# The delta rule's merge gates in column pairs: seven block products for three of eight k-tile pairs, in turn with the up blocks

## Chip, cores and metric

One core of one Trainium2 chip runs the whole program. The metric is device time in microseconds (us) of that core, given as the median of several executions; one further execution was taken with the hardware profiler, and all rows below come from it.

## What is computed

One layer of a hybrid decoder trunk over 256 tokens, width 2048, in float32. Cut to what matters here:

```
xn = RMSNorm(x)                      z = xn @ W_in
y_m = mLSTM(z_m)   y_r = RWKV7(z_r)  y_s = S5(z_s)
mixed = sig(g_m)*(y_m @ U_m) + sig(g_r)*(y_r @ U_r) + sig(g_s)*(y_s @ U_s)
h = x + mixed @ W_out
h = h + (silu(hn @ W_g) * (hn @ W_u)) @ W_d          # hn = RMSNorm(h)
h = h + (p @ W_ple) * sig(RMSNorm(h) @ W_pg)         # then a last RMSNorm
```

The change is about `g_r`, the 2048 gate columns of z that weigh the delta rule's (RWKV7's) branch. They are one product of a 256x2048 activation with a 2048x2048 weight.

## The kernel before

Every large product is done in two parts per operand: an operand is split into a rounded high part (a ScalarE copy) and the rest (a VectorE subtraction), and three TensorE matmuls (high by high, low by high, high by low) stand for one product. Weights come in chunks of four 128x512 tiles, 1 MB each, in the fixed order of `wall` through a ring of three `raw` tiles on SP's DMA queue; `chunk` splits a chunk into two pairs of `whi` and `wlo` tiles, of which there are three each, under high priority. `gemm_tm` makes one block of 512 output columns for both halves of the tokens (`t` is 0 or 1): for each of 16 k-tiles and each half three matmuls of 128x512, so 24 matmuls a chunk, into two PSUM tiles of the pool `mm` (four tiles). Everything else that TensorE writes (the small products and the transposes) goes into PSUM tiles of the pool `sm` (`psm()`, four tiles as well).

SBUF tiles of one tag share a number of buffers: `t2` has 16 of 128x512 (`b2`), `t8` two of 128x2048 (`b8`; at this place `KR` and then `UV`), `t4` twelve (`b4`), and the pool `pb` one each of `Dm`, `cm`, `X`, `XT` and `Y`, used by `rw_inverse` alone.

The order on each engine is made at build time by a planner, which follows the order of the program as a priority, but lets an instruction of a later part go first where the earlier part waits. So the serial chain of the delta rule (`rw_kappa`, `rw_gram`, `rw_inverse`, four `rw_chunk`, `rw_norm`) is written ahead of the gates of `s` and `r`, and runs in small pieces between their matmuls. `rw_chunk` takes `pu`, `py`, `px` and (except in the last) `pst` from `sm`; `rw_norm` takes two `pq` (L1072) and two `pt` (L1079), and ends with `yrh` and `yrl`, which `up("r", n)` needs. Per block, `up` multiplies the gate with a product of four k-tiles and adds it to `mixed`; the result is transposed through `sm` and split into `mh` and `ml` for W_out.

The feed-forward part already does, for the gate and up columns of W_g and W_u, what the change does for `g_r`: for k-tile pairs u in `SEVEN` it replaces the eight block products of a 2x2 by 2x2 block scheme by seven products of sums (Strassen's scheme in Winograd's form). `seven()` makes the sums of weight blocks on GpSimd and VectorE and splits them, and the products that belong to several outputs are gathered in four more PSUM tiles, `M[1]`, `M[7]`, `M[5]` and `M[6]`, of the pool `sm`, from the first of these pairs to the last:

```
ORDER = (3, 4, 0, 5, 1, 6, 2, 7)
SEVEN = (0, 1, 2)
...
    if u == SEVEN[0]:
        for q in (1, 7, 5, 6):
            M[q] = psm("M%d" % q)
```

A pair of this kind takes 7 x 3 = 21 matmuls, any other 24.

Of the kernel before, what the change touches and what calls it, by code (L numbers as in the profile page):

```python
# [74 lines left out]
def trunk(ctx: ExitStack, tc: tile.TileContext, xT, x, pT, wall, vecs, csts, s5b, s5c, gfin, out, dbg=None):  # L75
# [142 lines left out]
    def tt(o, a, b, op):  # L218
        nc.vector.tensor_tensor(out=o, in0=a, in1=b, op=op)
# [513 lines left out]
    def z_gate(key, n):  # L733
        ps = gemm_tm(xh, xl, NKT)
        with tc.high_priority():
            for t in range(2):
                g_ = t2("gate")
                act_fn(g_, ps[t], AF.Tanh, scale=hrs0[:, t:t + 1])
                gates[key, t, n] = g_

    def up(key, n, hi, lo, nkt, first):
# [396 lines left out]
    for n in range(4):  # L1138
        z_gate("s", n)
        up("s", n, lambda k: G["ysh"][:, k, :], lambda k: G["ysl"][:, k, :], 4, False)  # L1140
    for n in range(4):
        z_gate("r", n)
    mT = {}
    for n in range(4):
        up("r", n, lambda k: G["yrh"][:, k, :], lambda k: G["yrl"][:, k, :], 4, False)
        mh = t4v(4, "mh").bitcast(F32R)
        ml = t4v(4, "ml").bitcast(F32R)
        mT[n] = (mh, ml)
        for b in range(2):
            pt = tposed([mixed[t, n] for t in range(2)], 2 * b)  # L1150
            split(mh[:, 2 * b:2 * b + 2, :], ml[:, 2 * b:2 * b + 2, :], bank2(pt), 0.5)
# [49 lines left out]
    SF = {}
    for u in SEVEN:
        af = t2("af").rearrange("p (a t) -> p a t", a=2)  # L1210
        sf = t2("sf").rearrange("p (a t) -> p a t", a=4)
        tt(af, hh[:, 2 * u:2 * u + 2, :].bitcast(F32), hl[:, 2 * u:2 * u + 2, :].bitcast(F32), ALU.add)
        tt(sf[:, 0], af[:, 0, TS[1]], af[:, 1, TS[1]], ALU.add)
        tt(sf[:, 1], sf[:, 0], af[:, 0, TS[0]], ALU.subtract)
        tt(sf[:, 2], af[:, 0, TS[0]], af[:, 0, TS[1]], ALU.subtract)
        tt(sf[:, 3], af[:, 1, TS[0]], sf[:, 1], ALU.subtract)
        SF[u] = tuple(gu.tile([128, 4, 128], F32R, name=q + "%d" % u) for q in ("sh", "sl"))
        split(*SF[u], sf)

    def tiled(r):  # L1220

        n = r.shape[1]
        hi = ring.tile([128, 2, 512], F32R, name="whi", tag="whi", bufs=3)[:, 0:n]
        lo = ring.tile([128, 2, 512], F32R, name="wlo", tag="wlo", bufs=3)[:, 0:n]
        split(hi, lo, r)
        return [(hi[:, q], lo[:, q]) for q in range(n)]

    def seven():

        if not loaded:  # L1230
            load()
        raw, _ = loaded.pop(0)
        with tc.high_priority():
            ts_ = gu.tile([128, 3, 512], F32, name="tsum", tag="tsum", bufs=2)
            out_ = [tiled(raw[:, 0:2])]
            nc.gpsimd.tensor_tensor(out=ts_[:, 0], in0=raw[:, 3], in1=raw[:, 0], op=ALU.subtract)
            tt(raw[:, 3], raw[:, 2], raw[:, 3], ALU.subtract)
            out_.append(tiled(raw[:, 2:4]))
            tt(ts_[:, 1], raw[:, 3], raw[:, 0], ALU.add)
            nc.gpsimd.tensor_tensor(out=ts_[:, 2], in0=raw[:, 1], in1=ts_[:, 1], op=ALU.subtract)  # L1240
            out_ += [tiled(ts_[:, 0:2]), tiled(ts_[:, 2:3])]
        return out_

    def A(u, t, k):
        return hh[:, 2 * u + k, TS[t]], hl[:, 2 * u + k, TS[t]]

    for b in range(11):
        M = {q: pmm() for q in (2, 4, 3, 8)}
        done = set()

        def prods(ops, last):

            n_ = {q: max(i for i, o in enumerate(ops) if o[0] == q) for q in {o[0] for o in ops}}
            for part in range(2):
                for i, (q, a, w) in enumerate(ops):
                    mm2(M[q], *a, *w, part, q not in done, last and part == 1 and i == n_[q], True)
                    if part == 0:
                        done.add(q)

        for i, u in enumerate(ORDER):  # L1260
            last = u == ORDER[-1]
            if u in SEVEN:
                if u == SEVEN[0]:
                    for q in (1, 7, 5, 6):
                        M[q] = psm("M%d" % q)
                (b11, b21), (b22, t3), (t1, t2_), (t4_,) = seven()
                S = [tuple(SF[u][q][:, i_, :] for q in range(2)) for i_ in range(4)]
                end = u == SEVEN[-1]
                prods([(1, A(u, 0, 0), b11)], end)
                prods([(2, A(u, 0, 1), b21)], last)  # L1270
                prods([(3, S[3], b22)], last)
                prods([(7, S[2], t3)], end)
                prods([(5, S[0], t1)], end)
                prods([(6, S[1], t2_)], end)
                prods([(4, A(u, 1, 1), t4_)], last)
                if end:

                    with tc.high_priority():
                        m1, u2, u3, u4, v4 = (t2(q) for q in ("m1s", "u2", "u3", "u4", "v4"))
                        nc.scalar.copy(out=m1, in_=M[1])  # L1280
                        tt(u2, M[6], m1, ALU.add)
                        tt(u3, M[7], u2, ALU.add)
                        tt(u4, M[5], u2, ALU.add)
                        tt(v4, M[5], u3, ALU.add)
            else:
                b11, b21, b22, b12 = chunk()
                prods([(2, A(u, 0, 0), b11), (4, A(u, 1, 0), b11), (2, A(u, 0, 1), b21), (4, A(u, 1, 1), b21)], last)
                prods([(3, A(u, 0, 0), b12), (8, A(u, 1, 0), b12), (3, A(u, 0, 1), b22), (8, A(u, 1, 1), b22)], last)
        with tc.high_priority():
            for o, q in ((m1, 2), (u3, 4), (u4, 3), (v4, 8)):  # L1290
                tt(o, M[q], o, ALU.add)
        sg = []
        for t, (g_, u_) in enumerate(((m1, u4), (u3, v4))):
# [93 lines left out]
def layout(i):  # L1387
# [62 lines left out]
    wg, wu = (a[q][0].reshape(8, 2, 128, FFN) for q in ("ffn_w_gate", "ffn_w_up"))  # L1450
    for n in range(11):
        c = slice(n * 512, (n + 1) * 512)
        for u in ORDER:
            chunks.append(np.stack([wg[u, 0, :, c], wg[u, 1, :, c], wu[u, 1, :, c], wu[u, 0, :, c]], axis=1).reshape(128, 2048))
    blocks(a["ffn_w_down"][0])
    wp = a["ple_w_proj"][0]
    for n in range(4):
# [42 lines left out]
```

## Time and profile before

| | |
|---|---|
| median of 3 runs | 1662.36 us (1661.29 to 1663.82) |
| the profiled execution | 1665.54 us |
| its span, first to last instruction | 1663.8 us |
| mean granted TensorE clock | 0.997 |
| busy: TensorE, VectorE, ScalarE, GpSimd | 1643.1, 1269.2, 911.3, 173.5 us |
| mean DMA rate | 189 GB/s |

Times in a row are us from the start of the span, unless marked ns. L and a number is a line of the kernel before. A duration of a matmul is its time through the array, which overlaps the next one; the pace is the distance between starts. A merged row (x4) has its first start and the length of the whole. What stands in square brackets is the idle time of the engine ahead of the instruction and what ended it.

### The profile page before, as it was taken

The page shows a single profiled execution, that of the slowest core. Times are in us where ns is not written, and L with a number is a line of the kernel's source. Part 1 is how long each engine was busy: PE and PEld are TensorE (multiplying, and loading weights), DVE is VectorE, ACT ScalarE, POOL GpSimd, SP SyncE. Part 2 cuts the span into 40 slices and gives each one's busy share as a digit, 9 for nine tenths or more (in the row PEclk, how much of TensorE's full clock was granted, in tenths as well). Part 3 has the DMA queues.
Part 4 walks back from the last instruction along what each step waited for, and adds up shares of the span by engine and source line. Part 5 has one row for each costly group of instructions (what it writes and reads, how often), then busy time and mean ns, then how long its engine had stood idle before and what let it go on. Part 6 is the DMA issues. An engine that isn't in the chain of part 4 may idle for free. (4 is left out here: it accounts for less than half of the span.)

```text
span 1663.8 us, 23495 instructions
## 1 busy us (share of the span) xinstructions
PE 1643.1 (99%) x9255; PEld 1383.7 (83%) x9255; DVE 1269.2 (76%) x1566; ACT 911.3 (55%) x1142; POOL 173.5 (10%) x131
## 2 busy tenths in 40 slices
PE   8999999999999999999999999999999999999997
PEld 7999879988788878888888888888888888888886
DVE  6999776969988546565588889898888867666565
ACT  6465466556645444444555555555555656655454
POOL 1100100100000000000032222222222000000000
PEclk9999999999999999999999999999999999999999
DMA  9655444654554444555544555555555655555653
GB/s 356 197 174 177 160 162 177 191 189 170 188 177 152 154 153 154 183 197 200 202 174 181 203 202 203 202 190 191 193 189 198 230 186 199 181 199 184 220 186 119
DMA packets 49455, 313.69 MB, mean 189 GB/s; under 512 B 5824, under 2 KB 9152, under 8 KB 12736
## 3 DMA queue, kind: packets, MB, share of 16 engines
q1 hardware_dynamic: 43488, 304.59, 50.7%
q0 software_dynamic: 3840, 3.15, 1.1%
q10 hardware_dynamic: 2016, 4.46, 0.8%
q8 instruction: 72, 1.18, 0.3%
q14 instruction: 39, 0.32, 0.1%
HBM read 306.93 MB, written 2.10 MB: 186 GB/s over the span
## 5 line engine op out<-in xcount | busy, mean ns | idle before, releaser
L129 DVE TENSOR_TENSOR wlo<-raw,whi 128x1024 fp32r<-128x1024 f32 (+1 forms) x496 | 631.1, 1280 | 252.2 <-ACT whi L128 222.1
L128 ACT CAST whi<-raw 128x1024 fp32r<-128x1024 f32 (+1 forms) x496 | 517.7, 1049 | 553.9 <-PE mm L143 402.6
L143 PE MATMUL mm<-whi,alo 128*128 128x512 f32 x512 | 202.0, 394 | 0.0
L142 PE MATMUL mm<-whi,ahi 128*128 128x512 f32 x512 | 201.7, 394 | 0.0
L142 PE MATMUL mm<-whi,hhi 128*128 128x512 f32 x506 | 199.2, 394 | 0.4 <-ACT whi L193 0.2
L143 PE MATMUL mm<-whi,hlo 128*128 128x512 f32 x506 | 196.9, 390 | 0.0
L149 PE MATMUL mm<-ahi,whi 128*128 128x256 f32 x576 | 143.4, 286 | 7.8 <-ACT whi L128 7.8
L145 PE MATMUL mm<-wlo,hhi 128*128 128x512 f32 x506 | 146.0, 392 | 0.1
L150 PE MATMUL mm<-alo,whi 128*128 128x256 f32 x576 | 142.8, 285 | 0.3 <-DVE alo L197 0.3
L145 PE MATMUL mm<-wlo,ahi 128*128 128x512 f32 x512 | 139.6, 393 | 0.0
L142 PE MATMUL mm<-whi,dh 128*128 128x512 f32 x352 | 130.4, 390 | 0.0
L143 PE MATMUL mm<-whi,dl 128*128 128x512 f32 x352 | 130.2, 389 | 0.0
L149 PEld LDWEIGHTS mm<-ahi,whi 128*128 128x128 f32 x576 | 111.4, 194 | 8.9 <-ACT whi L128 8.1
L142 PEld LDWEIGHTS mm<-whi,hhi 128*128 128x128 f32 x506 | 95.0, 188 | 25.1 <-issue 4.1
L143 PEld LDWEIGHTS mm<-whi,alo 128*128 128x128 f32 x512 | 96.6, 189 | 21.1 <-issue 1.2
L142 PEld LDWEIGHTS mm<-whi,ahi 128*128 128x128 f32 x512 | 96.4, 188 | 21.3 <-issue 1.2
L145 PEld LDWEIGHTS mm<-wlo,ahi 128*128 128x128 f32 x512 | 96.0, 189 | 20.8 <-issue 0.4
L150 PEld LDWEIGHTS mm<-alo,whi 128*128 128x128 f32 x576 | 111.3, 194 | 0.9 <-DVE alo L197 0.5
L145 PEld LDWEIGHTS mm<-wlo,hhi 128*128 128x128 f32 x506 | 94.1, 188 | 20.1 <-DVE wlo L129 1.0
L143 PEld LDWEIGHTS mm<-whi,hlo 128*128 128x128 f32 x506 | 95.1, 188 | 18.7
L193 ACT CAST whi<-raw 128x1024 fp32r<-128x1024 f32 x66 | 69.3, 1050 | 66.9 <-DVE wlo L129 33.4
L145 PE MATMUL mm<-wlo,dh 128*128 128x512 f32 x352 | 95.9, 391 | 0.0
(532 smaller groups left out, 2779.0 us busy)
## 6 DMA issues: line engine op xcount, KB each, us to landing
raw<-in_wall SPq DMA_DIRECT2D x283, 1024.0 KB, 4.8
xrow<-in_x SPq DMA_DIRECT2D x2, 1024.0 KB, 9.6
h<-in_x ACTq DMA_DIRECT2D x8, 256.0 KB, 3.2
xraw<-in_xT SPq DMA_DIRECT2D x3, 512.0 KB, 11.0
ub<-Bh POOLq DMA_DIRECT2D x16, 64.0 KB, 3.8
ub<-uh POOLq DMA_DIRECT2D x16, 64.0 KB, 3.8
gft<-in_gfin ACTq DMA_DIRECT2D x1, 1024.0 KB, 7.0
out_dram<-fin SPq DMA_DIRECT2D x4, 256.0 KB, 3.2
```

The lines of the kernel that those rows point to most:

```text
L128: nc.scalar.copy(out=hi[:, q, :], in_=r)
L129: nc.vector.tensor_tensor(out=lo[:, q, :], in0=r, in1=hi[:, q, :].bitcast(F32), op=ALU.subtract)
L142: nc.tensor.matmul(ps, ah, wh, start=first, stop=False, skip_group_check=skip)
L143: nc.tensor.matmul(ps, al, wh, start=False, stop=False, skip_group_check=skip)
L145: nc.tensor.matmul(ps, ah, wl, start=False, stop=last, skip_group_check=skip)
L149: nc.tensor.matmul(ps, wh, ah, start=first, stop=False, skip_group_check=skip)
L150: nc.tensor.matmul(ps, wh, al, start=False, stop=False, skip_group_check=skip)
L193: nc.scalar.copy(out=hi, in_=src)
```

## The change

`gemm_pair` is the feed-forward part's block taken out as a function, with the sums of activations (`sums_of`), the weights' sums (`seven`) and the seven products beside it; the feed-forward part now calls it. `z_gate2("r", n, XS)` uses it for the gates of two blocks of 512 columns, `n` and `n + 1`, instead of `z_gate("r", n)` for one. The order of the program becomes: the sums `XS` of the activations for three k-tile pairs, gates of blocks 0 and 1, up of 0 and 1, gates of 2 and 3, up of 2 and 3; before it was gates 0 to 3, then up 0 to 3. The weights lie in `wall` in that order. The sums of activations are kept in `rw_inverse`'s buffers of `pb`, the sums of weights in `t8` buffers. The number of chunks and bytes is the same.

```
+    def room_pb(i):
+        t_ = [G["pb"].tile([128, 512], F32, name="sx", tag=q) if q else t2("sx") for q in (("Dm", "cm"), ("X", "XT"), ("Y", None))[i]]
+        return tuple(q.rearrange("p (a t) -> p a t", a=4).bitcast(F32R) for q in t_)
+    def tsum_t8():
+        return t8("tsum").rearrange("p a t -> p (a t)")[:, 0:1536].rearrange("p (a t) -> p a t", a=3)
...
+    def seven(room):
...
+            ts_ = room()
+            out_ = [tiled(raw[:, 0:2])]
+            nc.gpsimd.tensor_tensor(out=ts_[:, 0], in0=raw[:, 3], in1=raw[:, 0], op=ALU.subtract)
+            tt(raw[:, 3], raw[:, 2], raw[:, 3], ALU.subtract)
+            out_.append(tiled(raw[:, 2:4]))
+            tt(ts_[:, 1], raw[:, 3], raw[:, 0], ALU.add)
+            nc.gpsimd.tensor_tensor(out=ts_[:, 2], in0=raw[:, 1], in1=ts_[:, 1], op=ALU.subtract)
+            out_ += [tiled(ts_[:, 0:2]), tiled(ts_[:, 2:3])]
...
+    def gemm_pair(A, S, order, by7, room, prep=None, onto=None):
+        M = {q: pmm() for q in (2, 4, 3, 8)}
...
+            if u in by7:
+                if u == by7[0]:
+                    for q in (1, 7, 5, 6):
+                        M[q] = psm("M%d" % q)
+                (b11, b21), (b22, t3), (t1, t2_), (t4_,) = seven(room)
+                end = u == by7[-1]
+                prods([(1, A(u, 0, 0), b11)], end)
+                prods([(2, A(u, 0, 1), b21)], last)
+                prods([(3, S(u, 3), b22)], last)
+                prods([(7, S(u, 2), t3)], end)
+                prods([(5, S(u, 0), t1)], end)
+                prods([(6, S(u, 1), t2_)], end)
+                prods([(4, A(u, 1, 1), t4_)], last)
...
+    def z_gate2(key, n, sf):
+        c4 = gemm_pair(act_of(ahi, alo), sum_of(sf), ORDER, SEVEN, tsum_t8)
+        with tc.high_priority():
+            for o, (t, m) in zip(c4, ((0, n), (1, n), (0, n + 1), (1, n + 1))):
+                act_fn(o, o, AF.Tanh, scale=hrs0[:, t:t + 1])
+                gates[key, t, m] = o
...
-    for n in range(4):
-        z_gate("r", n)
+    XS = {u: sums_of(ahi[:, 2 * u:2 * u + 2, :], alo[:, 2 * u:2 * u + 2, :], room_pb(u)) for u in SEVEN}
     mT = {}
     for n in range(4):
+        if n % 2 == 0:
+            z_gate2("r", n, XS)
         up("r", n, lambda k: G["yrh"][:, k, :], lambda k: G["yrl"][:, k, :], 4, False)
...
-    blocks(w_in[:, 8648:10696])
-    blocks(a["w_up_r"][0])
+    for n in (0, 1024):
+        pair(w_in[:, 8648 + n:9160 + n], w_in[:, 9160 + n:9672 + n], ORDER)
+        blocks(a["w_up_r"][0][:, n:n + 1024])
```

## Rows read from the trace of the kernel before

**Rows 1.** Busy time of each engine in stretches of 20 us around the gates of `r` (length; then PE, PEld, DVE, ACT and POOL busy us with their instructions; granted TensorE clock, DMA share, GB/s).

```profile
640.00:660.00 20.00, 20.00 (x113) 16.00 (x112) 12.71 (x14) 8.97 (x12) 2.05 (x1) 1.00 0.38 130
...
740.00:760.00 20.00, 20.00 (x101) 16.66 (x100) 16.06 (x21) 9.39 (x12) 0.00 (x0) 1.00 0.47 170
```

**Rows 2.** TensorE's instructions in order of time at the start of the gates of `r` (start, length, engine, line): the first matmul of the block `r`, 0; two first matmuls of half chunks of 12 matmuls; the pieces of the delta rule's last chunk between them; and the last pair of transposes of `rw_norm`.

```profile
625.16 0.39 PE L142 MATMUL mm<-whi,ahi 128*128 128x512 f32 x1
...
632.49 0.39 PE L142 MATMUL mm<-whi,ahi 128*128 128x512 f32 x1
...
635.21 0.39 PE L142 MATMUL mm<-whi,ahi 128*128 128x512 f32 x1
...
636.21 1.15 PE L1017 MATMUL sm<-ST,KR 64*64 64x64 f32 x32
637.29 0.69 PE L1023 MATMUL sm<-UV,GB 128*64 128x64 f32 x16
...
639.86 0.40 PE L142 MATMUL mm<-whi,ahi 128*128 128x512 f32 x1
...
642.91 0.68 PE L1035 MATMUL sm<-Up,NX 64*64 64x64 f32 x16
643.52 1.99 PE L1072 MATMUL sm<-mur,ct 128*128 128x256 f32 x8
...
667.40 2.08 PE L1079 MATMUL sm<-ct,Yr 64*64 64x64 f32 x64
```

**Rows 3.** The same chain on ScalarE, in order of time.

```profile
638.02 0.37 ACT L1031 COPY Up<-sm 128x256 f32<-128x256 f32 x1 [2.42 <-PE sm L1023]
...
643.64 0.37 ACT L1036 COPY UV<-sm 64x256 f32<-64x256 f32 x1 [0.70 <-PE sm L1035]
...
649.83 0.37 ACT L1052 COPY Yr<-sm 128x256 f32<-128x256 f32 x1 [1.61 <-PE sm L1023]
...
653.01 1.06 ACT L225 ACTIVATE ysq<-Yr 128x1024 f32<-128x1024 f32 x1 [0.78 <-DVE Yr L219]
...
674.42 1.05 ACT L193 CAST yrh<-yrF 128x1024 fp32r<-128x1024 f32 x1 [0.90 <-DVE yrF L219]
```

**Rows 4.** The same chain on VectorE, in order of time.

```profile
650.23 1.22 DVE L1058 TENSOR_REDUCE st<-Yr 128x16 f32<-128x1024 f32 x1 [0.76 <-ACT Yr L1052]
651.48 0.17 DVE L214 TENSOR_SCALAR st<-st 128x16 f32<-128x16 f32 x1
651.69 1.23 DVE L219 TENSOR_TENSOR Yr<-Yr,st 128x1024 f32<-128x1024 f32 x1
...
655.29 1.21 DVE L1063 TENSOR_REDUCE st<-ysq 128x16 f32<-128x1024 f32 x1
...
661.77 1.23 DVE L219 TENSOR_TENSOR Yr<-Yr,grs 128x1024 f32<-128x1024 f32 x1
...
675.50 1.23 DVE L194 TENSOR_TENSOR yrl<-yrF,yrh 128x1024 fp32r<-128x1024 f32 x1
```

**Rows 5.** GpSimd's instructions in order of time: the clearing of `UV`, the power in `rw_norm`, and the first sum of weights of the feed-forward part.

```profile
520.82 1.95 POOL L900 MEMSET UV<- 64x1024 f32 x2 [151.23 <-PE sm L896]
657.95 3.79 POOL L1066 TENSOR_TENSOR grs<-st,nhalf 128x16 f32<-128x16 f32 x1 [135.18 <-ACT whi L128]
839.18 1.29 POOL L1236 TENSOR_TENSOR tsum<-raw 128x512 f32<-128x512 f32 x1 [177.44 <-PE mm L145]
```

**Rows 6.** The instructions that write or read a tile, with minimum, median and maximum of their ns, and the first and last start: `mur` from 480 us on, and `muv` in the whole span.

```profile
L1072 PE MATMUL sm<-mur,ct x8: 379/379/483, 643.5 to 645.1; 128*128 128x256 f32 x8
L222 DVE SCALAR_TENSOR_TENSOR mur<-mur,vt,muk x4: 478/478/484, 505.0 to 506.2; 128x256 f32<-128x256 f32 x4
...
L906 PE MATMUL sm<-ct,muv x64: 218/218/267, 522.2 to 524.1; 64*64 64x64 f32 x64
...
L222 DVE SCALAR_TENSOR_TENSOR muv<-zp,vt,muv x4: 478/479/480, 343.6 to 346.6; 128x256 f32<-128x256 f32 x4
```

**Rows 7.** The chain that ended last, in order of time (start, us, what): the same merged piece of two successive blocks of the feed-forward part, each with three pairs by seven products.

```profile
860.79 0.91 PE mm L145 x4
...
903.52 0.91 PE mm L145 x4
```

**Rows 8.** Groups of VectorE instructions in one such block, 860 to 903 us (line, engine, operation, shapes, count; busy us, mean ns; idle time before them).

```profile
L194 DVE TENSOR_TENSOR wlo<-raw,whi 128x1024 fp32r<-128x1024 f32 x6 | 8.2, 1379 | 1.0 <-PE mm L145 1.0
L194 DVE TENSOR_TENSOR wlo<-tsum,whi 128x1024 fp32r<-128x1024 f32 (+1 forms) x6 | 6.4, 1077 | 2.0 <-PE mm L145 1.9
L219 DVE TENSOR_TENSOR raw<-raw 128x512 f32<-128x512 f32 x3 | 2.1, 685 | 1.2 <-POOL tsum L1236 1.2
L219 DVE TENSOR_TENSOR tsum<-raw 128x512 f32<-128x512 f32 x3 | 2.0, 681 | 0.0
```

**Rows 9.** The one stretch after the start with a low granted clock (columns as in rows 1).

```profile
165.00:170.00 5.00, 5.00 (x18) 3.77 (x17) 3.88 (x8) 0.28 (x1) 0.00 (x0) 0.75 0.64 210
170.00:172.00 2.00, 2.00 (x9) 1.33 (x8) 0.32 (x1) 1.59 (x2) 0.00 (x0) 0.78 0.00 0
```

**Rows 10.** TensorE in order of time around the same stretch.

```profile
164.13 1.99 PE L644 MATMUL sm<-gw,sel 4*128 4x256 f32 x8
...
168.02 0.63 PE L143 MATMUL mm<-whi,alo 128*128 128x512 f32 x1
168.45 0.63 PE L142 MATMUL mm<-whi,ahi 128*128 128x512 f32 x1
```

More of the change, by code (lines that the diff above doesn't have):

```diff
@@ L197, in split, with sums, sums_of @@
             nc.vector.scalar_tensor_tensor(out=lo, in0=src, scalar=gain, in1=hi.bitcast(F32), op0=ALU.mult, op1=ALU.subtract)
+    def sums(sf, a):
+        tt(sf[:, 0], a[:, 0, TS[1]], a[:, 1, TS[1]], ALU.add)
+        tt(sf[:, 1], sf[:, 0], a[:, 0, TS[0]], ALU.subtract)
+        tt(sf[:, 2], a[:, 0, TS[0]], a[:, 0, TS[1]], ALU.subtract)
+        tt(sf[:, 3], a[:, 1, TS[0]], sf[:, 1], ALU.subtract)
+    def sums_of(hi, lo, room):
+        af = t2("af").rearrange("p (a t) -> p a t", a=2)
+        sf = t2("sf").rearrange("p (a t) -> p a t", a=4)
+        tt(af, hi.bitcast(F32), lo.bitcast(F32), ALU.add)
+        sums(sf, af)
+        split(*room, sf)
+        return room
@@ new lines, in room_of, with tsum_of @@
+    def room_of(pool, name):
+        return tuple(pool.tile([128, 4, 128], F32R, name=name + q) for q in ("h", "l"))
+    def room_pb(i):
+        t_ = [G["pb"].tile([128, 512], F32, name="sx", tag=q) if q else t2("sx") for q in (("Dm", "cm"), ("X", "XT"), ("Y", None))[i]]
+        return tuple(q.rearrange("p (a t) -> p a t", a=4).bitcast(F32R) for q in t_)
+    def tsum_of(pool):
+        return lambda: pool.tile([128, 3, 512], F32, name="tsum", tag="tsum", bufs=2)
+    def tsum_t8():
+        return t8("tsum").rearrange("p a t -> p (a t)")[:, 0:1536].rearrange("p (a t) -> p a t", a=3)
@@ new lines, in tiled @@
+    def tiled(r):
+        n = r.shape[1]
+        hi = ring.tile([128, 2, 512], F32R, name="whi", tag="whi", bufs=3)[:, 0:n]
+        lo = ring.tile([128, 2, 512], F32R, name="wlo", tag="wlo", bufs=3)[:, 0:n]
+        split(hi, lo, r)
+        return [(hi[:, q], lo[:, q]) for q in range(n)]
+    def seven(room):
+        if not loaded:
+            load()
+        raw, _ = loaded.pop(0)
+        with tc.high_priority():
[7 more added lines that the diff above has]
+            out_ += [tiled(ts_[:, 0:2]), tiled(ts_[:, 2:3])]
+        return out_
@@ new lines, in act_of, with sum_of, prods @@
+    def act_of(hi, lo):
+        return lambda u, t, k: (hi[:, 2 * u + k, TS[t]], lo[:, 2 * u + k, TS[t]])
+    def sum_of(sf):
+        return lambda u, i: tuple(q[:, i, :] for q in sf[u])
+    def gemm_pair(A, S, order, by7, room, prep=None, onto=None):
+        M = {q: pmm() for q in (2, 4, 3, 8)}
+        done = set()
+        def prods(ops, last):
+            n_ = {q: max(i for i, o in enumerate(ops) if o[0] == q) for q in {o[0] for o in ops}}
+            for part in range(2):
+                for i, (q, a, w) in enumerate(ops):
+                    mm2(M[q], *a, *w, part, q not in done, last and part == 1 and i == n_[q], True)
+                    if part == 0:
+                        done.add(q)
+        for u in order:
+            last = u == order[-1]
+            if prep is not None:
+                prep(u)
+            if u in by7:
[11 more added lines that the diff above has]
+                prods([(4, A(u, 1, 1), t4_)], last)
+                if end:
+                    with tc.high_priority():
+                        m1, u2, u3, u4, v4 = (t2(q) for q in ("m1s", "u2", "u3", "u4", "v4"))
+                        nc.scalar.copy(out=m1, in_=M[1])
+                        tt(u2, M[6], m1, ALU.add)
+                        tt(u3, M[7], u2, ALU.add)
+                        tt(u4, M[5], u2, ALU.add)
+                        tt(v4, M[5], u3, ALU.add)
+                    res = (m1, u3, u4, v4)
+                    if onto is not None:
+                        for o, r in zip(onto, res):
+                            tt(o, o, r, ALU.add)
+                        res = onto
+            else:
+                b11, b21, b22, b12 = chunk()
+                prods([(2, A(u, 0, 0), b11), (4, A(u, 1, 0), b11), (2, A(u, 0, 1), b21), (4, A(u, 1, 1), b21)], last)
+                prods([(3, A(u, 0, 0), b12), (8, A(u, 1, 0), b12), (3, A(u, 0, 1), b22), (8, A(u, 1, 1), b22)], last)
+        with tc.high_priority():
+            for o, q in zip(res, (2, 4, 3, 8)):
+                tt(o, M[q], o, ALU.add)
+        return res
@@ L739, in z_gate @@
                 gates[key, t, n] = g_
+    def z_gate2(key, n, sf):
+        c4 = gemm_pair(act_of(ahi, alo), sum_of(sf), ORDER, SEVEN, tsum_t8)
+        with tc.high_priority():
+            for o, (t, m) in zip(c4, ((0, n), (1, n), (0, n + 1), (1, n + 1))):
+                act_fn(o, o, AF.Tanh, scale=hrs0[:, t:t + 1])
+                gates[key, t, m] = o
     def up(key, n, hi, lo, nkt, first):
@@ L1199, in trunk @@
     hh, hl = hT
[L1208 to L1242, printed above, removed]
@@ L1244, in A @@
-    def A(u, t, k):
-        return hh[:, 2 * u + k, TS[t]], hl[:, 2 * u + k, TS[t]]
-    for b in range(11):
[L1248 to L1291, printed above, removed]
@@ L1292, in trunk @@
+    SF = {u: sums_of(hh[:, 2 * u:2 * u + 2, :], hl[:, 2 * u:2 * u + 2, :], room_of(gu, "sf%d" % u)) for u in SEVEN}
+    for b in range(11):
+        c11, c21, c12, c22 = gemm_pair(act_of(hh, hl), sum_of(SF), ORDER, SEVEN, tsum_of(hid_p))
         sg = []
-        for t, (g_, u_) in enumerate(((m1, u4), (u3, v4))):
+        for t, (g_, u_) in enumerate(((c11, c12), (c21, c22))):
             s_ = t2("sg")
@@ L1430, in blocks, with pair @@
             block(w[:, n * 512:(n + 1) * 512])
+    def pair(l, r, order):
+        l, r = (q.reshape(-1, 2, 128, 512) for q in (l, r))
+        for u in order:
+            chunks.append(np.stack([l[u, 0], l[u, 1], r[u, 1], r[u, 0]], axis=1).reshape(128, 2048))
     block(w_in[:, 6088:6600])
@@ L1446, in layout @@
         block(a["w_up_s"][0][:, n * 512:(n + 1) * 512])
-    blocks(w_in[:, 8648:10696])
-    blocks(a["w_up_r"][0])
+    for n in (0, 1024):
+        pair(w_in[:, 8648 + n:9160 + n], w_in[:, 9160 + n:9672 + n], ORDER)
+        blocks(a["w_up_r"][0][:, n:n + 1024])
     blocks(a["w_out"][0])
-    wg, wu = (a[q][0].reshape(8, 2, 128, FFN) for q in ("ffn_w_gate", "ffn_w_up"))
     for n in range(11):
         c = slice(n * 512, (n + 1) * 512)
-        for u in ORDER:
-            chunks.append(np.stack([wg[u, 0, :, c], wg[u, 1, :, c], wu[u, 1, :, c], wu[u, 0, :, c]], axis=1).reshape(128, 2048))
+        pair(a["ffn_w_gate"][0][:, c], a["ffn_w_up"][0][:, c], ORDER)
     blocks(a["ffn_w_down"][0])
```

## The prediction

> **What bounds the kernel now.** I read the page first: TensorE is busy 99% of the span, no other engine over 76%. So a change is worth what it takes from TensorE's own list, less what it makes TensorE wait. The table by stretches then shows the stage itself: around the gates of `r` TensorE is busy 20.00 of 20 us, VectorE 12.7 and, among the up blocks, 16.1 [rows 1]. There is no idle time to win here, and any wait put in is paid in full. TensorE's order of time gives the pace: twelve 128x512 matmuls from 632.49 to 635.21 us, 0.2267 us each, so 5.44 us for a chunk of 24 [rows 2].
>
> The reader should see in the same rows what lies between these matmuls. The gates of `r` begin at 625.16 us, while the delta rule's chain is in its last chunk. Its pieces are short, but each waits for a ScalarE or VectorE step and then for the matmuls queued ahead of it: the copy of `Up` ends at 638.39 and L1035, which needs it, starts at 642.91, 4.5 us later [rows 2, 3]. The transposes of `rw_norm` (L1079) start at 667.40, and `yrl`, the last thing that the up blocks need, is done at 676.7 [rows 2, 4]. Before, that is early: four gate blocks come first. The gates of `r` are what fills TensorE while the chain runs.
>
> **The change part by part.**
>
> *Matmuls.* Two column pairs, each with three k-tile pairs at 21 instead of 24: 2 x 3 x 3 = 18 matmuls fewer, 18 x 0.2267 = **4.08 us less** [rows 2]. Nothing excludes the full gain: the feed-forward part does 183 such matmuls and eight transposes in 42.73 us a block [rows 7], where 183 x 0.2267 is 41.5, so the seven products run at the same pace.
>
> *The place of the four extra sums.* `M[1]`, `M[7]`, `M[5]`, `M[6]` come from the pool `sm`, which is also that of the chain. What matters is whether they may have a free tile while earlier parts of the program have not yet asked for theirs. The trace answers by tiles that were ready long before. L1072 needs only `mur`, written by 506.7 us, and a tile of `sm`; it ran at 643.52, straight behind L1035, which writes the last `sm` tile that the program asks for ahead of it. L906 needs only `muv`, written by 347.1 us, and ran at 522.2 [rows 2, 6]. Both have precedence over the gates' matmuls, and both let gate matmuls pass for over 100 us. I read this as: tiles of one pool are handed out in program order. (Not in order of age, though: `UV` waited 151 us for L896, the last reader of `BK`, and so took `BK`'s place and not `KR`'s [rows 5].) Then `M[1]` cannot be had before the second pair of `rw_norm`'s `pt` tiles is, that is before L1079.
>
> *What TensorE has left to do.* Chunks 3 and 4 of the first pair take the place of the first two chunks of `r`, 0, and end at 639.86 as those do [rows 2]. Of the chunk u=0, `M[2]` and `M[3]` can go, 6 matmuls, 1.36 us. `M[1]` waits, and holds the first of three `whi`/`wlo` pairs; `M[7]` holds the second, `M[5]` and `M[6]` the third, so `M[4]` has no weights, and neither has any later chunk. The up blocks need `yrh`. TensorE stands until the chain gets to L1079, apart from the chain's own pieces.
>
> *How long.* With TensorE empty the chain has no queue to wait in. `Up` ends at 638.4 [rows 3]; L1035 behind the rest of chunk 4 and `M[2]`, 640.5 to 641.2; the copies into `UV`, 0.4, hidden behind L1072's 2.0, to 643.2; L1023, 0.69, to 643.9; `Yr`, 0.37, to 644.3. Then `rw_norm`: 1.22 + 0.17 + 1.23 on VectorE, 1.06 on ScalarE, 1.21 + 0.17 on VectorE, 3.79 on GpSimd, 1.23 on VectorE, 10.08 in all [rows 3 to 5], and some 0.6 for the hand-overs (the gaps in these rows are 0.03 to 0.23): L1079 at 655.0. From 639.86 to there is 15.1 us, in which TensorE has 1.36 of the gates and 0.68 + 1.99 + 0.69 of the chain, 4.7 in all. **10.4 us idle.** Lower bound: L1035 starts as soon as `Up` is there and L1072 slips behind, L1079 at 651, 6.4 idle. Upper bound: the planner leaves the chain the waits that it has now; the last VectorE step ends at 663.0 [rows 4], 18.4 idle. I take 10.4, since the waits of now are made by matmuls that are then not there.
>
> *The clock behind the idle time.* The one low stretch of the trace follows eight thin matmuls (L644, 4 rows): matmuls start 0.43 us apart, the clock is at 1.2 GHz for part of it, 0.75 over 5 us and 0.78 over 2 us [rows 9, 10]. That lost 5 x 0.25 + 2 x 0.22 = 1.7 us. Eleven idle us are at least as quiet, so I take **1.7**, between 0 (no fall) and 3.4 (the doubled stretch). The Trainium skill says so in general (TensorE: Matmul & The Clock Gate, "HAM oscillation"): a wait between bursts of matmuls sends the array back to half rate and the next burst starts cold. By that rule the 1.7 is due, and the change's 18 saved matmuls are worth little beside one such wait; without a fall the sum would be 1.7 lower. No trace so far shows a wait of this kind.
>
> *Restart.* The third weight pair is free only after `M[5]` and `M[6]`; `M[4]`'s weights need a copy and a subtraction behind `M[1]`, while `M[7]`, `M[5]`, `M[6]` give 2 us of cover. **0.5**, from 0 to 2.
>
> *Edits at nothing.* A chunk of seven products costs VectorE (8.2 + 6.4 + 2.1 + 2.0) / 3 = 6.2 us [rows 8], some 3.8 more than a plain one: six of them 22 us over some 108 us, in which it idles 4 to 7 of every 20 [rows 1]. The sums `XS` (per pair two operations of 0.69 and four a quarter the size [rows 8]) fall under matmuls ahead of 639 us, since `rw_inverse`'s buffers are long free. The eight adds of 0.69 behind each pair lie under chunk 7 and the up blocks. If that cover goes, each us is paid once; behind the second pair, where VectorE is at 16 of 20 [rows 1], I allow up to 2 and take 0. GpSimd's sums, 1.29 each [rows 5], meet an engine that idled 135 us before the power; one of them could delay that power by 1.3, inside the upper bound. The first needs `KR`'s buffer, free at 637.4 after L1017 [rows 2]. SP issues as many chunks as before, in the new order. In the second pair `M[1]` waits for the transposes of up block 1, with two plain chunks, 10.9 us, ahead of it; the feed-forward part has its transposes ahead of `M[1]` likewise and loses nothing [rows 7]. Its own refactoring: nothing.
>
> *Sum:* -4.08 + 10.4 + 1.7 + 0.5 = **+8.5 us**. The profiled execution took 1665.54 us around a span of 1663.8; the median shown is 1662.36, 0.2% lower, and I set the difference on it: **1670.9**. By the bounds, +2.3 (-4.1 + 6.4) to +19.7 (-4.1 + 18.4 + 3.4 + 2): 1664.7 to 1682.
>
> **The rivals.** *First come, first served.* If a free `sm` tile goes to whoever is ready, `M[1]` starts at 640 and all four are held to the end of chunk 2. The chain goes on with what is left, which costs `M[5]` and `M[6]` about 0.9. But L1079 finds no tile until the sums are read out, and runs behind chunk 7. From the end of L1079 to `yrl` is now 669.5 to 676.7, 7.2 us, 1.2 of it behind another subtraction [rows 2, 4]; less two matmuls that can start, 5.5 idle ahead of up block 0. -4.08 + 0.9 + 5.5 = +2.3: **1664.7**. For it: the planner lets later work pass. Against it: rows 6.
>
> *No wait, faster.* If `M[1]` had its tile and L1079 too, the first pair would end at 625.16 + 41.5 + some 9.4 of the chain's pieces, 676, exactly when `yrl` is ready now [rows 2, 4]; the 4.08 stay: **1658.3**. It takes L1079 before `M[1]` is due at 640, or tiles for both. For it: rows 7. Against it: the chain is 15 us from L1079 at that point, by sums that no queue explains.
>
> *The chain keeps its waits.* As forecast, with the idle time near its upper bound because the split of weights and `XS` stand ahead of the chain on VectorE: **1680**.
>
> **How the numbers follow.** Forecast 0.62, first come 0.17, no wait 0.13, long wait 0.08. The range 1659 to 1679 leaves out the no-wait case (0.13) and part of the long one. A change of 0.2% is 3.3 us, about what a measurement here can tell. Faster: the no-wait case, 0.13. Same: nearly all of first come, with the forecast's low edge, 0.15. Slower: the rest, 0.72.
>
> **What the changed profile would show.** Right: 18 matmuls fewer; TensorE idle for some 10 us between 641 and 656, L1079 there, and M's L142 for the first pair only behind it; a low granted clock in that stretch; `yrl` well ahead of up block 0. First come: `M` matmuls before L1079, and the idle time ahead of the first `yrh` matmul, near 676. Wrong altogether: TensorE at 20.00 of 20 through the stage. The weakest step is the order of the pool, read from two operations; the next is the length of the chain once TensorE is free.

## The result: slower by 0.76%, inside the forecast's range

| | before | after |
|---|---|---|
| median | 1662.88 us of 4 runs (1661.29 to 1663.82) | 1675.91 us of 4 runs (1673.13 to 1676.25) |
| profiled execution, its span | 1665.54, 1663.8 us | 1676.25, 1674.5 us |
| mean granted TensorE clock | 0.997 | 0.992 |
| TensorE busy, matmuls | 1643.1 us, 9255 | 1641.3 us, 9237 |

The ratio is 1.0076, with a 95% interval from 1.0064 to 1.0088. The forecast was 1670.9, with a range from 1659 to 1679. Line numbers have moved: L1148 is the old L1017, L1154 is L1023, L1166 is L1035, L1183 is L1052, L1189 is L1058, L1203 is L1072, L1210 is L1079, L1197 is L1066, L254 and L258 are GpSimd's sums L1236 and L1240, and L342 and L348 are the helpers L219 and L225. The seven products are still recorded as L142, L143 and L145.

The first lines to read are the page's busy times, and the page's two slice rows for TensorE and its clock. 18 matmuls are gone, as the edit says, but one slice of 40 has TensorE at six tenths and the clock at seven.

```profile
PE 1641.3 (98%) x9237; PEld 1381.7 (83%) x9237; DVE 1306.1 (78%) x1624; ACT 922.4 (55%) x1159; POOL 194.6 (12%) x143
...
PE   8999999999999996999999999999999999999997
...
PEclk9999999999999997999999999999999999999999
```

The waits of TensorE from 600 to 760 us (engine, line, what it waited for; total, times, longest) say who ended that: the transposes of `rw_norm`, behind the last VectorE step of that chain. The table by stretches (columns as in [rows 1]) puts it between 640 and 660 us. After that TensorE is full again.

```profile
PE sm L1210 <- DVE Yr L342: 12.4, 1, 12.4
PE mm L145 <- DVE wlo L194: 0.5, 1, 0.5
```

```profile
640.00:660.00 20.00, 7.14 (x91) 5.80 (x90) 12.73 (x14) 4.58 (x7) 8.52 (x4) 0.62 0.16 53
660.00:680.00 20.00, 20.00 (x85) 16.34 (x85) 16.55 (x16) 13.14 (x15) 3.98 (x2) 0.96 0.32 124
740.00:760.00 20.00, 20.00 (x92) 16.25 (x91) 18.09 (x23) 11.01 (x13) 0.00 (x0) 1.00 0.66 237
```

TensorE in order of time shows the whole event; compare [rows 2].

```profile
636.06 0.39 PE L142 MATMUL mm<-whi,ahi 128*128 128x512 f32 x1
...
638.30 0.50 PE L145 MATMUL mm<-wlo,ahi 128*128 128x512 f32 x1
638.84 0.68 PE L1166 MATMUL sm<-Up,NX 64*64 64x64 f32 x16
639.45 1.99 PE L1203 MATMUL sm<-mur,ct 128*128 128x256 f32 x8
641.37 0.69 PE L1154 MATMUL sm<-UV,GB 128*64 128x64 f32 x16
641.99 0.50 PE L142 MATMUL mm<-whi,sx 128*128 128x512 f32 x1
642.32 0.40 PE L143 MATMUL mm<-whi,sx 128*128 128x512 f32 x1
643.19 0.50 PE L145 MATMUL mm<-wlo,sx 128*128 128x512 f32 x1 [0.47 <-DVE wlo L194]
656.08 3.68 PE L1210 MATMUL sm<-ct,Yr 64*64 64x64 f32 x64 [12.39 <-DVE Yr L342]
659.69 0.79 PE L142 MATMUL M<-whi,ahi 128*128 128x512 f32 x1
660.28 0.63 PE L143 MATMUL M<-whi,alo 128*128 128x512 f32 x1
660.71 0.63 PE L145 MATMUL M<-wlo,ahi 128*128 128x512 f32 x1
661.13 0.63 PE L142 MATMUL M<-whi,sx 128*128 128x512 f32 x1
```

`M[2]` (636.06 to 638.80) and `M[3]` (from 641.99), both in `mm`, run, then nothing for 12.39 us, then L1210, and only behind it the first matmul into `M[1]`. The first two lines shown are `M[2]`: from the start of the gates at 623.27 to 638.84 us there are 51 large matmuls, 48 of the two plain chunks and three more. `M[1]` stands ahead of `M[2]` in the program, and its weights are the other half of the same `whi` and `wlo` tiles. So at 638 us it lacked neither weights nor activations, only its tile in `sm`.

At the end of the wait the chain's transposes take 3.68 us instead of 2.08, and the five matmuls behind them take 2.21 us from start to start, 0.59 to 0.34 each. To put a number on the stage I measure from the last `gate` of `s` that ScalarE reads out (its first half, 617.20 before, 615.30 after) to the first `m1s` of the feed-forward part (875.16 and 885.51): 257.96 us before, 270.21 after. That is 12.25 of the 13.0 us between the medians. From there to the end the two profiles agree within 0.4 us.

### The profile page after: what moved, and what is told of

Read it like the earlier page. It is cut to its first block, busy times and chain, and to the rows that moved or that the text cites. A ratio compares the mean times of both kernels' runs of the same rounds, so it can differ in the third digit from the quotient of the medians.

```text
span 1674.5 us, 23585 instructions
## 1 busy us (share of the span) xinstructions
PE 1641.3 (98%) x9237; PEld 1381.7 (83%) x9237; DVE 1306.1 (78%) x1624; ACT 922.4 (55%) x1159; POOL 194.6 (12%) x143
## 5 line engine op out<-in xcount | busy, mean ns | idle before, releaser
L128 ACT CAST whi<-raw 128x1024 fp32r<-128x1024 f32 (+1 forms) x484 | 504.9, 1049 | 522.4 <-PE mm L143 363.3
L129 DVE TENSOR_TENSOR wlo<-raw,whi 128x1024 fp32r<-128x1024 f32 (+1 forms) x484 | 617.9, 1284 | 202.8 <-ACT whi L128 178.6
L142 PE MATMUL mm<-whi,hhi 128*128 128x512 f32 x506 | 199.3, 394 | 0.4 <-ACT whi L193 0.2
L143 PE MATMUL mm<-whi,hlo 128*128 128x512 f32 x506 | 197.0, 390 | 0.0
L142 PE MATMUL mm<-whi,ahi 128*128 128x512 f32 x476 | 187.8, 394 | 0.0
L143 PE MATMUL mm<-whi,alo 128*128 128x512 f32 x476 | 187.8, 394 | 0.0
L145 PE MATMUL mm<-wlo,hhi 128*128 128x512 f32 x506 | 146.0, 392 | 0.3 <-DVE wlo L129 0.3
L145 PE MATMUL mm<-wlo,ahi 128*128 128x512 f32 x476 | 131.8, 393 | 0.0
L142 PE MATMUL mm<-whi,dh 128*128 128x512 f32 x352 | 130.4, 390 | 0.1
L143 PE MATMUL mm<-whi,dl 128*128 128x512 f32 x352 | 130.2, 389 | 0.0
L193 ACT CAST whi<-raw 128x1024 fp32r<-128x1024 f32 x78 | 81.8, 1050 | 76.9 <-DVE wlo L129 34.9
L254 POOL TENSOR_TENSOR tsum<-raw 128x512 f32<-128x512 f32 x39 | 63.7, 1633 | 501.4 <-DMA raw<-in_wall 258.3
L142 PEld LDWEIGHTS mm<-whi,hhi 128*128 128x128 f32 x506 | 95.0, 188 | 25.0 <-issue 4.0
L145 PEld LDWEIGHTS mm<-wlo,hhi 128*128 128x128 f32 x506 | 94.0, 188 | 20.4 <-DVE wlo L129 1.2
L143 PEld LDWEIGHTS mm<-whi,hlo 128*128 128x128 f32 x506 | 95.1, 188 | 18.7
L142 PEld LDWEIGHTS mm<-whi,ahi 128*128 128x128 f32 x476 | 89.8, 189 | 20.0 <-issue 1.2
L143 PEld LDWEIGHTS mm<-whi,alo 128*128 128x128 f32 x476 | 89.9, 189 | 19.7 <-issue 1.2
L145 PEld LDWEIGHTS mm<-wlo,ahi 128*128 128x128 f32 x476 | 88.9, 188 | 19.2 <-issue 0.4
```

The costliest lines, as they stand in the source:

```text
L128: nc.scalar.copy(out=hi[:, q, :], in_=r)
L129: nc.vector.tensor_tensor(out=lo[:, q, :], in0=r, in1=hi[:, q, :].bitcast(F32), op=ALU.subtract)
L142: nc.tensor.matmul(ps, ah, wh, start=first, stop=False, skip_group_check=skip)
L143: nc.tensor.matmul(ps, al, wh, start=False, stop=False, skip_group_check=skip)
L145: nc.tensor.matmul(ps, ah, wl, start=False, stop=last, skip_group_check=skip)
```

## The experiments

The theory to test: tiles of the PSUM pool `sm` are handed out in the order of the program, so `M[1]` waits for `rw_norm`'s `pt`; TensorE, with nothing else to do, waits for a chain of short steps; and the clock falls. Rivals: the new order of the up blocks takes the cover away, whatever the pool does; or the seven products themselves are late. Below, the stage is the one just defined, and 257.96 and 270.21 us are its lengths in the kernels before and after. Every edit is made to the changed kernel. Where it changes the order of the chunks, the order of the weights in `wall` changes with it; that is not shown below.

### The new order with plain blocks

```
-    XS = {u: sums_of(...) for u in SEVEN}
...
-            z_gate2("r", n, XS)
+            z_gate("r", n)
+            z_gate("r", n + 1)
...
```

> The gates of r by single blocks with all eight products (24 matmuls a chunk), but in the changed order: gates 0 and 1, up 0 and 1, gates 2 and 3, up 2 and 3. No M tiles at all. Theory A (the wait comes from M[1] being queued behind rw_norm's tiles in the pool sm): TensorE doesn't wait, since yrl was ready at 676.7 and up block 0 is due at about 625 + 43.5 + 9.4 = 678; against the kernel before -1 to +2 us. Theory B (the wait comes from the up blocks, moved ahead of two gate blocks that covered the delta rule's chain): most of the loss stays, +8 to +13 us.

Measured: 1663.24 us against 1663.12 for the kernel before, ratio 0.9999 (0.9990 to 1.0008); the stage takes 257.98 us. No wait of TensorE stands in the list from 600 to 800 us. So the new order costs nothing: with two plain gate blocks ahead of the up blocks the chain is still in time. The idle time belongs to the seven products.

### Seven products in the second pair alone

```
+        if n == 0:
+            z_gate("r", 0)
+            z_gate("r", 1)
+        if n == 2:
+            XS = {...}
+            z_gate2("r", n, XS)
...
```

> Seven products in the second pair of column blocks only; the first pair by single blocks with eight. Theory A: rw_norm is over when the second pair begins, so its M tiles are free at once: 9 matmuls fewer, -2.0 us against before (-3 to 0), no wait of TensorE over 1 us. Theory C (the seven products themselves cost more than they save, by their sums on VectorE and GpSimd): half of the loss stays with the one pair, +4 to +7 us.

Measured: 1663.11 us, ratio 0.9999 (0.9990 to 1.0008), stage 258.13. The long wait is gone with the first pair, and a loss of +4 to +7 is out. But the 2.04 us that nine matmuls are worth did not come either: the result lies at the edge of the expected -3 to 0, with a wait just over 1 us. TensorE's waits and one stretch (columns as in [rows 1]):

```profile
PE M L142 <- DVE ml L197: 1.1, 1, 1.1
```

```profile
700.00:720.00 20.00, 18.88 (x83) 15.06 (x82) 17.77 (x19) 10.95 (x11) 5.54 (x3) 1.00 0.50 172
```

VectorE is busy for 18.82 and 17.77 of 20 us in the two stretches from 680 us on, and TensorE waits for it once, 1.1 us. I also added up the distances between the starts of successive large matmuls in the stage, kernel by kernel. Those over 0.33 us, the wait among them, exceed the pace of 0.2267 by 1.7 us more in all than before; 16 more than before lie from 0.232 to 0.33 us, which makes 0.4 us; the rest adds 0.1. So the nine matmuls are paid back in pauses, about half of it in pauses too short to stand in the list of waits.

### The chain's normalisation behind the seven products

```
-    rw_norm()
...
     for n in range(4):
         if n % 2 == 0:
             z_gate2("r", n, XS)
+        if n == 0:
+            rw_norm()
```

> The changed kernel with rw_norm written behind the gates of the first pair instead of ahead of them, so that the four M tiles come before rw_norm's tiles in the program. Theory A: M[1] starts at about 641 straight after the plain chunks, the 12.4 us wait for L1079 is gone, and a smaller one appears ahead of up block 0, because rw_norm's matmuls now get their tiles only when the M sums are read out: 5 to 9 us and up to 2 for the clock, so +2 to +7 us against before. If the order of the program does not hand out the tiles (first come, first served), nothing moves: +12 to +14.

Measured: 1673.20 us, ratio 1.0057 (1.0043 to 1.0071), stage 268.04. The program's order alone is changed, and with it who waits. TensorE in order of time:

```profile
638.98 0.50 PE L142 MATMUL M<-whi,ahi 128*128 128x512 f32 x1
...
656.55 0.50 PE L142 MATMUL mm<-whi,ahi 128*128 128x512 f32 x1 [1.94 <-ACT whi L193]
656.89 0.56 PE L143 MATMUL mm<-whi,alo 128*128 128x512 f32 x1
657.25 0.63 PE L145 MATMUL mm<-wlo,sx 128*128 128x512 f32 x1
...
670.85 1.02 PE L1203 MATMUL sm<-mur,ct 128*128 128x256 f32 x4
...
677.48 2.08 PE L1210 MATMUL sm<-ct,Yr 64*64 64x64 f32 x64
685.31 2.08 PE L142 MATMUL mm<-whi,yrh 128*128 128x512 f32 x4 [5.75 <-ACT yrh L193]
```

`M[1]` now starts at 638.98, straight behind the plain chunks and `M[2]`, and L1210 follows the whole pair, at 677.48. L1203 is the clearest: it needs only `mur`, written by 504.4 us here, and a tile of `sm`. It did not run in the 1.94 us in which TensorE had nothing to do, but at 670.85, behind the copy that reads out `M[1]` (668.32). That is the pool's rule, seen from the other side: whoever is first in the program has the tiles, and the other waits until they are given back. The direction was as expected, the price was not: +10 instead of +2 to +7. The wait for `yrh` is 5.75 us as worked out for the rival, but VectorE also gets behind (18.81 of 20 us between 640 and 660 us), and TensorE runs at half clock twice, behind the 1.94 us wait and behind this one (granted 0.50 from 657 to 659 and from 685 to 691 us). The edit also moves `rw_norm` back in the order of the other engines, so this price is not the pool's alone.

### One more step in the chain

```
+        grs0 = pb.tile([128, 16], F32, name="grs0")
+        nc.gpsimd.tensor_tensor(out=grs0, in0=st[:, 1, :], in1=nhalf, op=ALU.pow)
```

(ahead of the power in `rw_norm`; its result is used by nothing)

> The changed kernel with the power of rw_norm done twice on GpSimd, one behind the other (the first result is not used): about 2.9 to 3.8 us more in the chain ahead of L1079. Theory A: the chain's length sets the wait, so TensorE waits 15.3 to 16.2 instead of 12.4 us, +15.5 to +17 us against before. If something else released TensorE (the weights' sums, a load), the time stays at +13.

Measured: 1677.71 us, ratio 1.0083 (1.0068 to 1.0099), stage 273.17, which is 2.96 more than without the edit. GpSimd in order of time, and TensorE's wait (L1212 is the old L1079 here):

```profile
651.55 2.94 POOL L1198 TENSOR_TENSOR grs<-st,nhalf 128x16 f32<-128x16 f32 x1 [1.60 <-DVE st L339]
654.47 2.89 POOL L1199 TENSOR_TENSOR grs<-st,nhalf 128x16 f32<-128x16 f32 x1
```

```profile
PE sm L1212 <- DVE Yr L342: 15.3, 1, 15.3
```

2.89 us more in the chain, 2.88 us more wait (15.27 against 12.39): the chain's length is the wait, one for one. The wait is as expected; the time is not, +14.6 us against the expected +15.5 to +17. The medians are of four runs each, here 1674.76 to 1678.60 us, so the reading rests on the profile.

### Seven products last in the first pair

```
+LATE = (3, 4, 5, 6, 0, 1, 2, 7)
...
-            z_gate2("r", n, XS)
+            z_gate2("r", n, XS, LATE if n == 0 else ORDER)
...
```

> The changed kernel with the k-tile pairs of the first column pair in the order 3, 4, 5, 6, 0, 1, 2, 7: two more plain chunks, 10.9 us, ahead of the first pair by seven products. Theory A: M[1] is due at about 652 instead of 641, but with TensorE full until then the delta rule's chain is slower too (Yr at about 649 as before the change, L1079's line some 13 us later), so the wait shrinks from 12.4 to about 9 us and the time against before from +13 to +6 to +10. If the wait were a fixed cost of starting the sevens, it would stay at +13.

Measured: 1673.36 us, ratio 1.0065 (1.0051 to 1.0078), stage 269.44. With two more plain chunks ahead of `M[1]` the wait is shorter, but by 3.5 us and not by the 10.9 us that the chunks last, since the chain waits in the queue behind them again:

```profile
PE sm L1211 <- DVE Yr L343: 8.9, 1, 8.9
PE M L146 <- DVE wlo L195: 2.2, 2, 1.6
```

What it gains is spent: three chunks by seven products stand one behind the other, and VectorE's splits are late for them twice. The wait of about 9 was as expected; the time, some 0.5 us above the +6 to +10, was not.

### Seven products in the second pair, further from the up blocks

```
+LATE = (3, 4, 5, 0, 6, 1, 2, 7)
...
+        if n == 0:
+            z_gate("r", 0)
+            z_gate("r", 1)
+        if n == 2:
+            z_gate2("r", n, XS, LATE)
...
```

> As e2_second_pair (sevens in the second column pair alone), but with a third plain chunk ahead of the first seven (order 3, 4, 5, 0, 6, 1, 2, 7) and the activation sums written ahead of the gates. Theory: what e2_second_pair lost of its 2.0 us is the 1.1 us wait of an M tile for the transposed mixed blocks of the up part, which are ahead of it in the same pool, and work on VectorE at that place; with 5.4 us more until the tile is due the wait is gone: -2.0 us against before (-2.6 to -1). If the sevens cost as much as they save even without a wait, 0.

Measured: 1661.95 us, ratio 0.9994 (0.9985 to 1.0003), stage 257.17. This is the best of the kernels tried, and it can't be told from the kernel before; the expected -2.6 to -1 is missed. TensorE's listed waits are 0.2 and 0.2 us, so the wait of 1.1 us was only a part of the loss. By the distances between starts, 0.8 us of the 2.04 go into pauses over 0.33 us, 0.3 into 13 more matmuls from 0.232 to 0.33 us and 0.2 into the rest; what is left is the 0.8 us that the stage shows. The order of the chunks and the place of the sums `XS` were changed together, and no run tells them apart.

### Seven products at W_out

W_out has no serial chain beside it. One kernel adds them there to the kernel just described, and another has them there alone, with plain gates:

```
+    for n in (0, 2):
...
+        gemm_pair(m_of, sum_of(XO), LATE, SEVEN, tsum_t8, onto=(h[0, n], h[1, n], h[0, n + 1], h[1, n + 1]))
+        for m in (n, n + 1):
+            h_block(m, hT, "gffn", ssq1)
...
```

> e7_second_late, and the product with W_out by two column pairs as well, three of eight k-tile pairs by seven products in the same order, added onto x. There the pool sm is asked for by nothing but the transposes of mixed and h. 9 + 18 = 27 matmuls fewer: -6.1 us, if no wait appears; with waits of 1 us at each of the three starts -3.

> The kernel before (gates of r by blocks, 0 to 3, then up 0 to 3) with only the product with W_out by column pairs and sevens: 18 matmuls fewer as in the change, but at a place where no serial chain is ahead of the M tiles in their pool. Theory A: -4.1 us less small waits, -4.1 to -2. If sevens with their sums do not pay outside the feed-forward part, 0 or slower.

Measured: 1667.40 us, ratio 1.0028 (1.0018 to 1.0038), and 1671.09 us, ratio 1.0051 (1.0038 to 1.0063). Both miss: the stage is 2.9 and 8.0 us longer than before. TensorE's longest waits and one stretch of the first:

```profile
PE sm L1303 <- DVE h L343: 4.5, 3, 3.3
PE mm L144 <- DVE sf0l L195: 2.6, 1, 2.6
```

```profile
820.00:840.00 20.00, 16.11 (x74) 12.69 (x73) 20.00 (x25) 10.85 (x18) 1.55 (x1) 1.00 0.54 205
```

VectorE is full there, and in the second kernel it is busy for 19.53 us between 840 and 860, with TensorE at 17.10 and a granted clock of 0.83. From the program I read why, though no run takes it apart: the blocks of `h` come two at a time, so the sums of both, their splits and the feed-forward part's own sums of activations (`sf0l`) come in one heap, and the transposes (L1303) wait for them. No long chain is needed for this loss.

### The first sums of weights on VectorE instead of GpSimd

The forecast's idle time was 2.5 us short. In the changed kernel VectorE's order of time shows where the chain lost time, in the two subtractions ahead of the first reduction:

```profile
641.18 1.95 DVE L194 TENSOR_TENSOR wlo<-raw,whi 128x1024 fp32r<-128x1024 f32 x1
643.06 2.29 DVE L194 TENSOR_TENSOR wlo<-tsum,whi 128x1024 fp32r<-128x1024 f32 x1
645.27 1.20 DVE L1189 TENSOR_REDUCE st<-Yr 128x16 f32<-128x1024 f32 x1
646.39 0.68 DVE L342 TENSOR_TENSOR raw<-raw 128x512 f32<-128x512 f32 x1
646.99 0.16 DVE L337 TENSOR_SCALAR st<-st 128x16 f32<-128x16 f32 x1
647.17 0.69 DVE L342 TENSOR_TENSOR tsum<-raw 128x512 f32<-128x512 f32 x1
```

`Yr` was there at 642.49 (ScalarE's L1183), and the reduction began at 645.27. Such a subtraction takes 1.23 us elsewhere [rows 4]. GpSimd, in order of time, in the same stretch:

```profile
640.77 1.28 POOL L258 TENSOR_TENSOR tsum<-raw,tsum 128x512 f32<-128x512 f32 x1 [1.60 <-DVE tsum L342]
642.15 2.11 POOL L254 TENSOR_TENSOR tsum<-raw 128x512 f32<-128x512 f32 x1
```

The second of these is already the first sum of the next chunk, u=1. The times interlock. The first subtraction would be through 1.1 us after GpSimd's first sum (642.05 to 643.13), the second sum 1.1 us after that subtraction (643.13 to 644.26), the second subtraction 1.1 us after that sum (644.26 to 645.35). I read: they go one at a time. The Trainium skill says it (SBUF — State Buffer, "SBUF: two separate sides"): a VectorE operation with two SBUF inputs and a GpSimd operation that reads SBUF exclude each other for the whole instruction. To test it, the first pair's sums for u=0 go to VectorE:

```
-            nc.gpsimd.tensor_tensor(out=ts_[:, 0], in0=raw[:, 3], in1=raw[:, 0], op=ALU.subtract)
+            (tt if vec else gp)(ts_[:, 0], raw[:, 3], raw[:, 0], ALU.subtract)
...
-            nc.gpsimd.tensor_tensor(out=ts_[:, 2], in0=raw[:, 1], in1=ts_[:, 1], op=ALU.subtract)
+            (tt if vec else gp)(ts_[:, 2], raw[:, 1], ts_[:, 1], ALU.subtract)
...
```

> The changed kernel, but the two sums of weights that GpSimd makes for the first pair by seven products (the first pair of column blocks, u=0) are made by VectorE, 0.69 us each. In the changed kernel VectorE's two subtractions there, wlo<-raw and wlo<-tsum, took 1.95 and 2.29 us instead of 1.23, with GpSimd's sums running beside them, and the first reduction of rw_norm, which stands behind them, started at 645.27. Theory (the two engines block each other on operations with two operands): with no such sum beside them the subtractions take 1.2 us again; VectorE does four sums of 0.62, two subtractions of 1.15 and the copy of 0.43 from about 637.9 on, so the reduction starts near 643.5, L1210 near 654.4, and TensorE's wait is 10.7 instead of 12.4; the time is 1674.2 against 1675.9. Rival (the subtractions were slow for another reason, such as their operands or the weights' transfers): they stay at 1.9 to 2.3, VectorE has 1.3 us more to do ahead of the reduction, the wait is 12.4 to 13.5 and the time 1676 to 1677.

Measured: 1672.82 us, ratio 1.0058 (1.0040 to 1.0076), stage 267.73. VectorE, then TensorE, in order of time:

```profile
640.62 1.22 DVE L194 TENSOR_TENSOR wlo<-raw,whi 128x1024 fp32r<-128x1024 f32 x1
641.87 0.43 DVE L1168 COPY UV<-sm 64x256 f32<-64x256 f32 x1
642.33 1.23 DVE L194 TENSOR_TENSOR wlo<-tsum,whi 128x1024 fp32r<-128x1024 f32 x1
643.68 1.22 DVE L1189 TENSOR_REDUCE st<-Yr 128x16 f32<-128x1024 f32 x1
```

```profile
654.50 3.67 PE L1210 MATMUL sm<-ct,Yr 64*64 64x64 f32 x64 [11.26 <-DVE Yr L342]
658.10 0.50 PE L142 MATMUL M<-whi,ahi 128*128 128x512 f32 x1
658.44 0.39 PE L143 MATMUL M<-whi,alo 128*128 128x512 f32 x1
```

The subtractions take 1.22 and 1.23 us. VectorE has two instructions more to do, and still the chain is 1.6 us earlier: the reduction at 643.68 for an expected 643.5, L1210 at 654.50 for 654.4. The rival is out. Two things were not as expected. The sum that had held the second subtraction, that of u=1, was not moved by the edit: its buffer came free later, so it ran from 643.38, beside the reduction, which has one input only, and neither was slower for it (1.29 and 1.22 us). And `Yr` itself came only at 643.65, since `M[3]`'s matmuls slipped in ahead of L1154's, so the wait is 11.26 and not 10.7. The stage fell by more than the waits (1.6 with the 0.47 us wait of `M[3]`, which is gone), 2.48 us, because the clock was back by the first matmul into `M[1]` here: 658.10 to 659.37 us for five starts, against 659.69 to 661.90.

## Why the prediction came out right, point by point

**The order of the pool** was called the weakest step, and holds: `M[1]` waited for L1079 in the changed kernel, and with the program's order reversed the tiles went the other way (the kernel with `rw_norm` behind). That settles the rivals. First come, first served would have had `M[1]` at 640, and the wait ahead of up block 0; there `yrh` was ready at 664.95 and its first matmul ran at 690.5. No wait, faster: the plain blocks in the same order have no wait, the seven products have one of 12.39. A third reading, that the planner merely set L1079 ahead of the gates by precedence, does not fit: `M[2]`, written behind `M[1]`, was let past both at 636.06.

**Matmuls:** 18 fewer, 4.08 us, as worked out.

**The idle time** was 10.4 and is 12.39 + 0.47. `M[2]` and `M[3]` ran ahead of `M[1]`, as worked out, and the matrix `Yr` was there on time: 27.2 us into the stage, for a forecast of 27.1 (644.3 less 617.20). The term that was too small is the chain from there: 13.6 us to L1079 (642.49 to 656.08), for a forecast of 10.7. I had given the splits of weights a price (VectorE has room) but no place. They stood ahead of the chain on VectorE, and with GpSimd's sums beside them two of them took 4.2 us instead of 2.5; so the first reduction waited 2.78 us. Two sums of the next chunk's weights, at 646.39 and 647.17, came between its steps and cost 1.2 more. The power took 2.94 us and not 3.79, which hid 0.85 of the miss, by luck. The last experiment takes the reduction's wait away (0.03 us) and gets 1.6 us at L1079, because `Yr` is 1.2 later there. The rival called "the chain keeps its waits" had named this cause, the splits ahead of the chain, with an idle time near 18.4. The lower and the upper bound, 6.4 and 18.4, hold.

**The clock** was 1.7 and is about 2.7: 1.6 in L1210's own 64 transposes, which I had left out, and 1.1 in the five matmuls from 659.69 to 661.90 (2.21 us, for 5 x 0.2267). The granted clock is 0.50 from 656 to 660 us. The rule of the Trainium skill that the prediction weighed (TensorE: Matmul & The Clock Gate, "HAM oscillation") agrees with this trace: the granted clock is 0.62 in the stretch of the wait, and 1.00 in the same stretch before [rows 1].

**Restart:** 0.5 was allowed. With the terms measured the stage comes to -4.1 + 12.9 + 2.7 = +11.5, and it is 12.25 longer. By the distances between starts, 0.7 of the 0.75 us between lies in 30 more matmuls than before from 0.232 to 0.33 us: many small delays and no second wait. What causes them isn't pinned down.

**Edits at nothing:** right for the order of the up blocks, for GpSimd's first sum (it starts at 637.90, for a forecast of 637.4) and for the sums `XS`, which TensorE did not wait for. Not right for the second pair, where I allowed up to 2 us and took 0: with that pair alone nothing of its 2.04 us came, or 0.8 of it with the seven products further from the up blocks and `XS` made earlier. How much of this is in the 0.75 can't be told, since no run has the first pair alone.

In all, the stage is 3.75 us longer than the forecast's +8.5: 2.5 from the wait, 1.0 from the clock and 0.25 from the rest. All three were taken too small, so the forecast did not come out by errors that cancel. The other 0.8 of the 13.0 between the medians lies outside it, and the start of the program alone differs by more than that between the two profiles (the stage begins at 617.20 and 615.30).

## What to carry to other kernels

When work is moved into a stretch that serves as cover, list every tile it needs and find which earlier part of the program has yet to ask for one of the same pool: an in-order pool turns a chain that nobody waited for into the bound. Price the moved work on each engine by its place in the queue too, not by its sum alone, and look for a second engine that it makes run against the first. A saving of matmuls counts only where VectorE has the sums that replace them done in time, and its busy share alone doesn't tell: the feed-forward part does its seven products with VectorE at 15.3 to 19.4 of 20 us and TensorE at 19.99 or more (960 to 1020 us before), the second pair at 17.8 to 18.8 only broke even, and at W_out, where VectorE was at 19.5 to 20, they cost more than they saved.

## What the runs showed of the hardware that I had not expected

VectorE's 128x1024 subtractions went from 1.23 to 1.95 and 2.29 us, and GpSimd's 128x512 sum from 1.28 to 2.11, with the other engine's beside them. The subtractions went back to 1.22 and 1.23 without, and a reduction with one input beside such a sum slowed neither (1.22 and 1.29). The power of 128x16 shows the same: 2.94 and 2.89 us with VectorE idle, 3.79 in the kernel before [rows 5], where it started at 657.95, in the middle of the first VectorE instruction below, which is through at 658.93; the difference is about the time left of it. But the exclusion did not last for the whole of that power: a second subtraction, from 660.43, took its usual 1.23 us. VectorE before, in order of time:

```profile
657.71 1.22 DVE L129 TENSOR_TENSOR wlo<-raw,whi 128x1024 fp32r<-128x1024 f32 x1
660.43 1.23 DVE L129 TENSOR_TENSOR wlo<-raw,whi 128x1024 fp32r<-128x1024 f32 x1 [1.49 <-ACT whi L128]
```

A short wait was followed by the lower clock, which I had only bounded by a stretch without a wait [rows 9, 10]. In the kernel with `rw_norm` behind, the matmuls that follow the wait of 1.94 us soon start 0.43 us apart, with a granted clock of 0.50, which is 1.2 GHz, from 657 to 659 us; there had been stops of 0.53 and 0.58 us 10 to 14 us ahead of it. In the kernel with the second pair alone the clock stayed at 1.00 from 703 to 705 us, behind a wait of 1.12.
